# The running sum of the 31-tap convolution on VectorE: in a PSUM bank instead of SBUF

## The chip, the core and the metric

The kernel runs on one core of one Trainium2 chip. The metric is the device time of one execution in microseconds (us); lower is better. TensorE multiplies, VectorE (DVE), ScalarE (ACT) and GpSimd (POOL) do the rest, SyncE (SP) issues most transfers. SBUF is the large on-chip memory, PSUM the smaller one of eight banks into which TensorE writes; one bank holds 128 x 512 numbers of fp32.

## The reference, cut to what matters

Two transformer blocks on 512 tokens of width 1024, in fp32. The change lies in the mixer of the first block, which runs an attention and a convolution side by side on the same normed input:

```python
q = rmsnorm(zq...); k = rmsnorm(zk...)            # 16 query heads, 2 key heads
a = sliding_window_attention(q, k, v, sinks[i]) @ attn_proj[i]
ca, cb = jnp.split(zc, 2, axis=-1)
u = ca * jax.nn.sigmoid(cb)
u = causal_depthwise_conv(u, dw_w[i], dw_b[i])    # 31 taps, each channel by itself
c = jax.nn.silu(layernorm(u, ...)) @ conv_proj[i]
merged = jax.nn.sigmoid(ga) * a + jax.nn.sigmoid(gb) * c
x = x + merged @ w_out[i]
```

For each of the 1024 channels the convolution is y[t] = b + sum over j of w[j] * u[t - 30 + j], 31 products and sums for each token.

## The kernel before

Activations lie with channels on the 128 partitions and the 512 tokens along the free dimension, so 1024 channels are 8 chunks. A weight matrix is used in units of 128 output channels. Each fp32 operand is split into a rounded part h and a rest l, and each product is three matmuls (`mm3`, lines L226 to L228: h by xh, h by xl, l by xh). A unit over 1024 inputs is therefore 24 matmuls of 512 columns. For each unit a weight block arrives in `wst` by a transfer, ScalarE casts it to `wh` (L187) and VectorE subtracts to get `wl` (L188); `wst` has two buffers, `wh` and `wl` have three each.

`mix` is the first mixer. Its units follow each other in the order in which the code is written: keys and values, then for each chunk c of the convolution a unit for cb and one for ca (16 units), then the 8 query chunks and the 8 second gates in turn (`MIX_ORDER`), then the 8 first gates, `attn_proj`, `conv_proj` and `w_out`. TensorE runs exactly in the written order. For VectorE, ScalarE and GpSimd a scheduler fixes the order when the kernel is built; at run time each engine goes through its own list and waits where an operand is not there.

The convolution's input `u` of a chunk is made by VectorE from the ca unit (L758). Then its 31 taps are handed out by `take`: so many at each unit (`FILL`), each not before the first matmuls of that unit. Chunks 0, 3 and 6 (`POOL_CONV`) go to GpSimd: ScalarE scales `u` into `cv` (L650), GpSimd adds it to `y` (L651). Chunks 1, 2, 4, 5 and 7 go to VectorE: one tap is one instruction (L654) that reads `u`, multiplies by a column of `vec` and adds the old `y`, which it reads from SBUF and writes back. Five taps of VectorE go with each of the 16 units, six with each gate unit of `MIX_ORDER`, seven with each first-gate unit. When all chunks are done, `layer_norm` begins.

Beside the 16 units of `MIX_ORDER` the attention runs in rounds, one after each unit (`attention`). A round has up to three parts for three different steps: `attn_c` (L617, probabilities by values, into a bank `sm`), `attn_b` (L604, two groups of transposes into two `pd` banks, each copied out by ScalarE into `pt`, L605) and `attn_a` (two groups of six matmuls of queries by keys into two more `pd` banks, each read by VectorE with the mask, L574; then three instructions on 4 columns, L579 to L581, and four exponentials on ScalarE, L583). Every second round also has the transposes of a query chunk (L516, one `pd` bank). PSUM is shared so: three banks `mm` for the units, one bank `sm`, and four banks `pd`, which the stage takes in turn.

Of the kernel before, what the change touches and what calls it, by code (L numbers as in the profile page):

```python
# [15 lines left out]
P = 128  # L16
S = 512
# [29 lines left out]

# queries and second gates in turn
MIX_ORDER = [0, 1]
# [4 lines left out]

# keys, queries and values of the attention to the memory
XA_ORDER = [("w_xk_2", m) for m in range(3)]
# [49 lines left out]
class Kern:  # L106
# [14 lines left out]

    # ---- tiles
    def nm(self, s):
# [16 lines left out]
    def pd(self):  # L140
        return self.pq.tile([P, S], F32, tag="pd", name=self.nm("pd"), bufs=4)

    def phase(self, name):
        """SBUF and PSUM of one stage; what it returns closes them."""
        ctx = ExitStack()
        self.pm = ctx.enter_context(self.tc.tile_pool(name=name, bufs=1))
        self.pq = ctx.enter_context(self.tc.tile_pool(name=name + "_ps", bufs=1, space=bass.MemoryType.PSUM))
        return ctx
# [12 lines left out]

    # ---- weight stream
    AHEAD_DMA, AHEAD_SPLIT, BOOST, MM = 4, 2, 400, 3
# [40 lines left out]

    # ---- background work
    def tick(self):
# [15 lines left out]

    # ---- matrix products
    def mm3(self, ps, h, l, xh, xl, first, last):
# [22 lines left out]
    def group(self, entries, xs, part, drain=False, fill=0):  # L247
        """Products whose last operands come late: each begins with xs[:part]."""
        begun = []
        for i, (name, m, evac) in enumerate(entries):  # L250
            self.mark(f"{name}/{m}")
            wh, wl = self.w_get(name, m)
            ps = self.mm()
            begun.append((wh, wl, ps, evac))
            for k in range(part):
                sl = slice(k * P, k * P + P)
                self.mm3(ps[:], wh[:, sl], wl[:, sl], *xs[k], k == 0, False)
                if k == 0 and fill:
                    self.take(fill, self.last_mm)
            with self.tc.high_priority(offset=self.BOOST):  # L260
                self.w_prefetch(max(1, min(self.AHEAD_SPLIT, 2 - i)))
            if drain:
                self.tick()
        if drain:
            self.drain()
        for wh, wl, ps, evac in begun:
            for k in range(part, len(xs)):
                sl = slice(k * P, k * P + P)
                self.mm3(ps[:], wh[:, sl], wl[:, sl], *xs[k], False, k == len(xs) - 1)
            with self.tc.high_priority(offset=self.BOOST):  # L270
                self.w_prefetch()
                evac(ps)
            if not drain:
                self.tick()

    def units(self, name, n, xs, first, part, evac, fill=0):
        """n products of one weight, of which some begin before the last operands."""
        if first:
            self.group([(name, m, lambda ps, m=m: evac(m, ps)) for m in range(first)], xs, part, True, fill)
        for m in range(first, n):  # L280
            self.unit(name, m, xs, lambda ps: evac(m, ps), fill=fill)

    # ---- arithmetic pieces
    def split(self, h, l, src, col=None):
# [9 lines left out]
    def rsqrt(self, ps, n, out, N=S, after=None):  # L294
        """out = (ps / n + EPS) ** -0.5: a first value from exp and ln, then a Newton step."""
        nc = self.nc
# [13 lines left out]
    def rsqrt_small(self, v, out, tag, after=None):  # L310
        """out = v ** -0.5 for a few columns."""
        nc = self.nc
# [10 lines left out]
    def preload(self, table, after, before):  # L323
        """Load an activation table between two instructions of ScalarE."""
        ld = self.nc.scalar.preload_act_table_set(table)
        self.order(ld, after)
        self.order(before, ld)
# [7 lines left out]
    def feed(self, acc, x, last, N=S):  # L335
        """Add the squares of one chunk to the accumulator acc (a list that holds its tile)."""
        nc = self.nc
# [16 lines left out]
    def norm_chunk(self, m, gname, last):  # L354
        """x chunk m is final: feed its square, and split x*g for the next product."""
        x = self.x[:, m, :]
# [20 lines left out]
    def lazy_R(self, acc, **k):  # L377
        """R is made where it is first asked for, when a first product is under way."""
        st = []
# [11 lines left out]

    # ---- stages
    def load(self, g0):
        """The first operands come in pieces, and before what only the norm needs."""
        nc = self.nc
# [21 lines left out]
    def ffn(self, tag, gnext, early=False):  # L417
        """early: the squares of x come late, so the first products are held until then."""
        nc = self.nc
# [39 lines left out]

    # ---- first mixer  # L460
    def spill_x(self):
# [28 lines left out]
    def rope_tables(self, a):  # L490
        """cos and sin times the gain of the queries."""
        nc = self.nc
# [6 lines left out]
    def q_chain(self, c, ps):  # L499
        """One chunk of queries without its norm, which q_scales gives to the scores."""  # L500
        nc = self.nc
# [22 lines left out]
    def q_scales(self, grp):  # L524
        """(mean(z^2) + EPS)^-0.5 / 8 for each place and head of a group."""
        nc = self.nc
# [111 lines left out]
    def conv_taps(self, c):  # L638
        """The convolution of one chunk of u, which comes doubled: mix halves the taps."""
        nc = self.nc  # L640
        u, y = self.u.pop(c), self.c5("y")[:, :S]
        w = lambda j: self.vcol("dw_w", c * 31 + j, 1)
        pool = c in self.POOL_CONV
        eng = nc.gpsimd if pool else nc.vector
        yield eng.tensor_scalar(out=y, in0=u[:, 30:542], scalar1=w(30), scalar2=self.vcol("dw_b", c),
                                op0=ALU.mult, op1=ALU.add)
        for j in range(30):
            if pool:
                t = self.t2("cv")
                r = nc.scalar.activation(t[:], u[:, j:j + S], AF.Copy, scale=w(j))  # L650
                eng.tensor_tensor(out=y, in0=y, in1=t[:], op=ALU.add)  # L651
                yield r
            else:
                yield eng.scalar_tensor_tensor(out=y, in0=u[:, j:j + S], scalar=w(j), in1=y,  # L654
                                               op0=ALU.mult, op1=ALU.add)
# [8 lines left out]
    def conv_fill(self, chunks):  # L664
        """The convolution of some chunks, a tap at a time."""
        for c in chunks:
# [4 lines left out]
    def take(self, counts, dep):  # L671
        """Up to so many taps of each filler, not before dep."""
        for fill, n in zip(self.fill, counts):
# [37 lines left out]
    def normed(self, gname, R):  # L711
        """Operands of the normed x itself, so that what its products give needs no scale."""
        nc = self.nc
# [8 lines left out]
    def mix(self, gnext):  # L722
        nc = self.nc
        ctx = self.phase("mixp")
        self.spill_x()
# [85 lines left out]

    # ---- gated embedding
    def ple(self, gnext):
# [33 lines left out]

    # ---- second mixer
    def bc(self, col, n):
        """[P, n] columns, each repeated over 128 places."""  # L850
        return col.rearrange("p (a c) -> p a c", c=1).to_broadcast([P, n, P])
# [51 lines left out]
    def conv4(self, raw, ch, out):  # L903
        """Causal convolution over 4 places of one chunk; raw has 3 zeros ahead."""
        nc = self.nc
# [6 lines left out]
    def token_squares(self, chunk, j):  # L912
        """Sum of one chunk's squares over the channels, a column for each block of 128 places."""
        nc = self.nc
# [11 lines left out]
    def dn_scales(self):  # L926
        """Scales of keys and queries, and what they make of the gates' columns."""
        tt = self.nc.vector.tensor_tensor
# [12 lines left out]
    def dn_chunk(self, n, st):  # L941
        """Decays, inverse of the triangle, and the products that one chunk of 128 places needs."""
        nc = self.nc
# [49 lines left out]
        def halves(t, l, odd):  # L993
            """The columns in even or odd blocks of 2^l."""
            w = 1 << l
# [114 lines left out]
    def dn_out(self, n, po):  # L1110
        """Norm and gate of one chunk's outputs, places on the partitions; then back to channels."""
        nc = self.nc
# [126 lines left out]

    # ---- attention to the memory  # L1240
    def xhead(self, h):
# [41 lines left out]
    def mem_prep(self):  # L1283
        """Operands and norm of the memory; the products that follow need no x."""
        nc = self.nc
# [69 lines left out]

    # ---- squared-relu MLP and the last norm
    def mlp(self):
# [21 lines left out]
    def final(self, hs):  # L1379
        """The last product by halves of the tokens: the norm of one is under way beside the other."""  # L1380
        nc = self.nc
# [73 lines left out]

# ---- host layout
def tile_w(w, k0=0, k1=None):
# [102 lines left out]
```

## Time and profile before

| | us |
|---|---|
| median of three runs | 2098.96 (2096.82 to 2099.27) |
| profiled execution, from its first to its last instruction (span) | 2092.0 |
| median less that span | 6.96 |
| TensorE busy over the span | 2015.6 |
| VectorE busy over the span | 1270.8 |
| first mixer, the part with taps on VectorE | 413.7 to 743.2 of the span |

The time of a run has some microseconds more than the span; the profiled execution has no time of its own beside its span here, so the median stands for it. A matmul's listed duration is longer than its distance to the next one (they overlap in the engine), so TensorE's busy share says little; its counts and the waits of a stretch say more. The three stretches used below are parts of the first mixer: 413.7 to 516.8 us, the units of ca and cb; 516.8 to 677.4 us, queries and second gates with the attention; 677.4 to 743.2 us, first gates with the last rounds of the attention.

### The profile page before, as it was taken

Reading aid. Unit: us, or ns where it says so; the run is one execution under the profiler, and the core shown is the slowest. Engines: PE = TensorE matmul, PEld = TensorE weight load, DVE = VectorE, ACT = ScalarE, POOL = GpSimd, SP = SyncE. Lnnn points to the kernel's source line nnn. Section 1 sums busy time; section 2 is a strip of 40 time slices with the busy share of each in tenths; the row PEclk is TensorE's granted clock in tenths of the full one; section 3 lists DMA queues with packets and bytes.
Section 4 is the critical chain, followed back from the end, with each engine's and each line's share of the span. In section 5 each row is a group of like instructions: output and inputs, shape, how many; then the busy total and the mean of one; then the engine's idle time right before and its main releaser. Section 6 shows DMA issues by size and latency. Waiting matters only on the chain. (4 is left out here: it accounts for less than half of the span.)

```text
span 2092.0 us, 25092 instructions
## 1 busy us (share of the span) xinstructions
PE 2015.6 (96%) x9564; PEld 1676.9 (80%) x9564; DVE 1270.8 (61%) x1956; ACT 876.8 (42%) x1465; POOL 249.3 (12%) x234
## 2 busy tenths in 40 slices
PE   8999999977899799999999999999999999999997
PEld 6888888756778578888888877788988988888886
DVE  6434345899989985544443468678486655344444
ACT  5323223633777652422222255354555444232233
POOL 0000000375223600000000002207100000000001
PEclk9999999998999899999999999999999999999999
DMA  5333333312212134332323224322034333233232
GB/s 178 100 94 98 101 92 122 103 61 71 79 60 79 41 96 132 130 100 92 101 92 100 91 82 145 100 86 72 7 117 146 119 103 101 91 101 97 95 101 71
DMA packets 65672, 201.13 MB, mean 96 GB/s; under 512 B 7312, under 2 KB 11536, under 8 KB 65424
## 3 DMA queue, kind: packets, MB, share of 16 engines
q1 hardware_dynamic: 64864, 199.00, 29.8%
q8 instruction: 76, 1.25, 0.2%
q10 hardware_dynamic: 688, 0.53, 0.1%
q14 instruction: 44, 0.36, 0.1%
HBM read 188.75 MB, written 10.49 MB: 95 GB/s over the span
## 5 line engine op out<-in xcount | busy, mean ns | idle before, releaser
L187 ACT CAST wh<-wst 128x1024 fp32r<-128x1024 f32 (+3 forms) x357 | 353.9, 992 | 934.1 <-PE mm L227 634.3
L226 PE MATMUL mm<-xh,wh 128*128 128x512 f32 x1272 | 502.2, 395 | 2.5 <-ACT xh L290 1.5
L228 PE MATMUL mm<-xh,wl 128*128 128x512 f32 x1272 | 495.9, 390 | 0.7 <-DVE wl L188 0.7
L227 PE MATMUL mm<-xl,wh 128*128 128x512 f32 x1272 | 495.4, 389 | 0.3 <-DVE xl L291 0.3
L188 DVE TENSOR_TENSOR wl<-wst,wh 128x1024 fp32r<-128x1024 f32 (+3 forms) x357 | 420.5, 1179 | 75.4 <-ACT wh L187 75.2
L226 PEld LDWEIGHTS mm<-xh,wh 128*128 128x128 f32 x1272 | 238.9, 188 | 55.0 <-issue 2.9
L227 PEld LDWEIGHTS mm<-xl,wh 128*128 128x128 f32 x1272 | 239.0, 188 | 52.2 <-issue 3.1
L228 PEld LDWEIGHTS mm<-xh,wl 128*128 128x128 f32 x1272 | 238.8, 188 | 51.5 <-DVE wl L188 1.6
L227 PE MATMUL mm<-hl,wh 128*128 128x512 f32 (+1 forms) x616 | 238.3, 387 | 0.2
L226 PE MATMUL mm<-hh,wh 128*128 128x512 f32 (+1 forms) x616 | 238.5, 387 | 0.0
L228 PE MATMUL mm<-hh,wl 128*128 128x512 f32 (+1 forms) x616 | 238.1, 387 | 0.0
L371 DVE SCALAR_TENSOR_TENSOR x<-mm,x 128x512 f32<-128x512 f32 x111 | 76.7, 691 | 248.7 <-PE mm L228 248.7
L651 POOL TENSOR_TENSOR y<-y,cv 128x512 f32<-128x512 f32 x90 | 143.4, 1594 | 158.4 <-ACT cv L650 153.8
L654 DVE SCALAR_TENSOR_TENSOR y<-u,vec,y 128x512 f32<-128x512 f32 x150 | 160.3, 1069 | 2.8
L228 PE MATMUL mm<-xnh,wl 128*128 128x512 f32 x304 | 123.4, 406 | 18.8 <-DVE wl L188 18.8
L227 PEld LDWEIGHTS mm<-hl,wh 128*128 128x128 f32 x616 | 115.7, 188 | 24.3 <-DVE hl L288 1.0
L226 PEld LDWEIGHTS mm<-hh,wh 128*128 128x128 f32 x616 | 115.7, 188 | 23.5
L228 PEld LDWEIGHTS mm<-hh,wl 128*128 128x128 f32 x616 | 115.7, 188 | 23.4
L226 PE MATMUL mm<-xnh,wh 128*128 128x512 f32 x304 | 124.0, 408 | 4.3 <-DVE u L758 3.6
L227 PE MATMUL mm<-xnl,wh 128*128 128x512 f32 x304 | 121.9, 401 | 0.0
L438 DVE TENSOR_TENSOR t<-mm,R 128x512 f32<-128x512 f32 x43 | 29.7, 692 | 138.4 <-PE mm L228 138.3
L228 PEld LDWEIGHTS mm<-xnh,wl 128*128 128x128 f32 x304 | 59.4, 195 | 35.3 <-DVE wl L188 22.4
(403 smaller groups left out, 2807.2 us busy)
## 6 DMA issues: line engine op xcount, KB each, us to landing
wst<-ffn_wgu SPq DMA_DIRECT2D x86, 512.0 KB, 3.5
wst<-w_in SPq DMA_DIRECT2D x63, 512.0 KB, 3.5
wst<-ffn_wdown SPq DMA_DIRECT2D x32, 512.0 KB, 3.5
wst<-w_up SPq DMA_DIRECT2D x32, 512.0 KB, 3.5
wst<-w_down SPq DMA_DIRECT2D x32, 512.0 KB, 3.5
wst<-ffn_wdown SPq DMA_DIRECT2D x16, 384.0 KB, 3.1
xd<-x SPq DMA_DIRECT2D x24, 256.0 KB, 2.3
x<-xd SPq DMA_DIRECT2D x24, 256.0 KB, 4.8
```

The lines of the kernel that those rows point to most:

```text
L187: r = self.nc.scalar.copy(h[:, c], st[:, c])
L188: self.nc.vector.tensor_tensor(out=l[:, c], in0=st[:, c], in1=h[:, c].bitcast(F32), op=ALU.subtract)
L226: self.last_mm = mm(ps, h, xh, start=first, stop=False)
L227: mm(ps, h, xl, start=False, stop=False)
L228: mm(ps, l, xh, start=False, stop=last)
L371: self.nc.vector.scalar_tensor_tensor(out=x, in0=ps[:], scalar=scale, in1=x, op0=ALU.mult, op1=ALU.add)
L438: nc.vector.tensor_tensor(out=t[:], in0=ps[:], in1=R[:], op=ALU.mult)
L651: eng.tensor_tensor(out=y, in0=y, in1=t[:], op=ALU.add)
L654: yield eng.scalar_tensor_tensor(out=y, in0=u[:, j:j + S], scalar=w(j), in1=y, op0=ALU.mult, op1=ALU.add)
```

## The change

On VectorE's five chunks the running sum is a tile `cacc` in PSUM. The first tap writes it, taps 2 to 30 read and write it, the last tap reads it and writes `y` in SBUF, which everything later uses as before. The bank comes from the stage's four `pd` banks, of which three are left in the first mixer; other stages keep four. GpSimd's chunks are as before. (The change also drops comments, which is not shown.)

```diff
     def pd(self):
-        return self.pq.tile([P, S], F32, tag="pd", name=self.nm("pd"), bufs=4)
+        return self.pq.tile([P, S], F32, tag="pd", name=self.nm("pd"), bufs=self.PD)
...
-    def phase(self, name):
...
-        ctx = ExitStack()
+    def phase(self, name, pd=4):
...
+        ctx, self.PD = ExitStack(), pd
...
     def conv_taps(self, c):
...
-        pool = c in self.POOL_CONV
-        eng = nc.gpsimd if pool else nc.vector
-        yield eng.tensor_scalar(out=y, in0=u[:, 30:542], scalar1=w(30), scalar2=self.vcol("dw_b", c),
-                                op0=ALU.mult, op1=ALU.add)
-        for j in range(30):
-            if pool:
...
-            else:
-                yield eng.scalar_tensor_tensor(out=y, in0=u[:, j:j + S], scalar=w(j), in1=y,
+        else:
+            eng = nc.vector
+            acc = self.pq.tile([P, S], F32, tag="cacc", name=self.nm("cacc"), bufs=1)[:]
+            yield eng.tensor_scalar(out=acc, in0=u[:, 30:542], scalar1=w(30), scalar2=self.vcol("dw_b", c),
+                                    op0=ALU.mult, op1=ALU.add)
+            for j in range(30):
+                yield eng.scalar_tensor_tensor(out=y if j == 29 else acc, in0=u[:, j:j + S], scalar=w(j), in1=acc,
                                                op0=ALU.mult, op1=ALU.add)
...
     def mix(self, gnext):
-        ctx = self.phase("mixp")
+        ctx = self.phase("mixp", 3)
```

The scheduler makes new lists for VectorE, ScalarE and GpSimd. First VectorE among the ca and cb units, where it goes from its first to its second chunk. Before:

```order
L654 SCALAR_TENSOR_TENSOR y_2849<-u_2841,vec,y_2849 128x512 x5
L758 SCALAR_TENSOR_TENSOR u_3127<-tcb_3035,mm_3082 128x512
L188 TENSOR_TENSOR wl_3172<-wst_3079,wh_3171 128x1024
L645 TENSOR_SCALAR y_3136<-u_2937,vec 128x512
L757 MEMSET u_3223 128x30
L654 SCALAR_TENSOR_TENSOR y_3136<-u_2937,vec,y_3136 128x512 x5
L188 TENSOR_TENSOR wl_3218<-wst_3125,wh_3217 128x1024
```

After the change, at the same place (lines stand five lower there, so L763 is the old L758):

```order
L659 SCALAR_TENSOR_TENSOR cacc_2850<-u_2841,vec,cacc_2850 128x512 x4
L763 SCALAR_TENSOR_TENSOR u_3128<-tcb_3036,mm_3083 128x512
L659 SCALAR_TENSOR_TENSOR cacc_2850<-u_2841,vec,cacc_2850 128x512
L188 TENSOR_TENSOR wl_3174<-wst_3080,wh_3173 128x1024
L659 SCALAR_TENSOR_TENSOR cacc_2850<-u_2841,vec,cacc_2850 128x512
L659 SCALAR_TENSOR_TENSOR y_2849<-u_2841,vec,cacc_2850 128x512
L762 MEMSET u_3225 128x30
L656 TENSOR_SCALAR cacc_3138<-u_2938,vec 128x512
L659 SCALAR_TENSOR_TENSOR cacc_3138<-u_2938,vec,cacc_3138 128x512 x2
L188 TENSOR_TENSOR wl_3220<-wst_3126,wh_3219 128x1024
```

The mix of taps and `wl` is the same, about five taps to a `wl`; the order shifts by a tap or two, and 58 taps stand ahead of the first query chunk in both lists.

Second TensorE in one round of the attention, whose order does not change but whose waits do (the name in brackets is the engine waited for). `pd` tiles are in the order two of `attn_b`, two of `attn_a`. Before:

```order
L604 MATMUL pd_4219<-cst,s_4025 128x128 [waits DVE_49] x2
L604 MATMUL pd_4225<-cst,s_4025 128x128 [waits Activation_49]
L604 MATMUL pd_4225<-cst,s_4025 128x128 x3
L226 MATMUL pd_4233<-kph,qh_3417 128x256 [waits DVE_49]
L227 MATMUL pd_4233<-kpl,qh_3417 128x256
L228 MATMUL pd_4233<-kph,ql_3418 128x256
L226 MATMUL pd_4242<-kph,qh_3417 128x256 [waits DVE_49]
```

After:

```order
L604 MATMUL pd_4222<-cst,s_4028 128x128 [waits DVE_49]
L604 MATMUL pd_4228<-cst,s_4028 128x128 [waits Activation_49]
L604 MATMUL pd_4228<-cst,s_4028 128x128 x3
L226 MATMUL pd_4236<-kph,qh_3419 128x256 [waits DVE_49]
L227 MATMUL pd_4236<-kpl,qh_3419 128x256
L228 MATMUL pd_4236<-kph,ql_3420 128x256
L226 MATMUL pd_4245<-kph,qh_3419 128x256 [waits Activation_49]
```

With four banks the second half of `attn_a` waited for VectorE, which had read the same bank a round earlier. With three it takes the bank of the round's own first `attn_b` transposes, so it waits for ScalarE to have copied them out.

## Rows read from the trace of the kernel before

**Rows 1.** The page: its first line, and all taps of VectorE (busy us, mean ns).

```profile
span 2092.0 us, 25092 instructions
...
L654 DVE SCALAR_TENSOR_TENSOR y<-u,vec,y 128x512 f32<-128x512 f32 x150 | 160.3, 1069 | 2.8
```

**Rows 2.** Busy time by stretch: start and end, length, then each engine.

```profile
core 0: us, PE busy (x) PEld busy (x) DVE busy (x) ACT busy (x) POOL busy (x), PEclk, DMA share, GB/s
413.70:516.80 103.10, 80.75 (x303) 62.25 (x302) 100.87 (x87) 38.80 (x56) 68.59 (x42) 0.88 0.20 61
516.80:677.40 160.60, 149.10 (x798) 128.14 (x797) 147.49 (x362) 120.07 (x271) 46.05 (x32) 0.98 0.23 75
677.40:743.20 65.80, 50.74 (x215) 40.65 (x213) 62.69 (x88) 36.28 (x77) 37.39 (x24) 0.90 0.15 47
...
410.50:427.00 16.50, 16.50 (x73) 13.44 (x73) 16.32 (x14) 9.67 (x14) 15.79 (x10) 1.00 0.21 64
```

**Rows 3.** Waits of TensorE, 413 to 517 us: total, times, longest.

```profile
PE mm L228 <- DVE wl L188: 18.8, 8, 5.8
```

**Rows 4.** Waits of TensorE, 516.8 to 677.4 us.

```profile
PE pd L516 <- ACT pt L605: 5.7, 4, 2.3
PE pd L604 <- ACT s L590: 3.2, 1, 3.2
```

**Rows 5.** Waits of TensorE, 677.4 to 743.2 us.

```profile
PE sm L617 <- ACT pt L605: 7.6, 2, 3.9
```

**Rows 6.** Groups of VectorE, 413.7 to 516.8 us: busy us, mean ns.

```profile
L654 DVE SCALAR_TENSOR_TENSOR y<-u,vec,y 128x512 f32<-128x512 f32 x58 | 72.6, 1252 | 1.6
L188 DVE TENSOR_TENSOR wl<-wst,wh 128x1024 fp32r<-128x1024 f32 x13 | 24.1, 1850 | 0.7 <-ACT wh L187 0.7
L758 DVE SCALAR_TENSOR_TENSOR u<-tcb,mm 128x512 f32<-128x512 f32 x6 | 4.1, 680 | 0.0
```

**Rows 7.** Timeline of VectorE about 430 us: start, us, what.

```profile
427.91 1.65 DVE L654 SCALAR_TENSOR_TENSOR y<-u,vec,y 128x512 f32<-128x512 f32 x1
429.48 0.67 DVE L758 SCALAR_TENSOR_TENSOR u<-tcb,mm 128x512 f32<-128x512 f32 x1
...
431.16 2.28 DVE L188 TENSOR_TENSOR wl<-wst,wh 128x1024 fp32r<-128x1024 f32 x1
```

**Rows 8.** Timeline of GpSimd: 17 additions without a gap.

```profile
407.56 30.39 POOL L651 TENSOR_TENSOR y<-y,cv 128x512 f32<-128x512 f32 x17
```

**Rows 9.** Durations of two lines: ns least/median/most.

```profile
L574 DVE CUSTOM_DVE_ANT_0 s<-pd,cst x64: 403/418/426, 535.8 to 703.9; 128x256 f32<-128x256 f32 x64
L291 DVE SCALAR_TENSOR_TENSOR xl<-x,vec,xh x56: 742/747/755, 5.1 to 1731.2; 128x512 fp32r<-128x512 f32 x56
L291 DVE SCALAR_TENSOR_TENSOR yp<-pd,vec,yp x4: 739/742/746, 1326.9 to 1343.5; 128x512 fp32r<-128x512 f32 x4
L654 DVE SCALAR_TENSOR_TENSOR y<-u,vec,y x150: 719/752/1880, 413.7 to 738.7; 128x512 f32<-128x512 f32 x150
```

**Rows 10.** Timeline of VectorE: three taps that follow each other.

```profile
509.94 2.31 DVE L654 SCALAR_TENSOR_TENSOR y<-u,vec,y 128x512 f32<-128x512 f32 x3
```

**Rows 11.** Groups of VectorE, 677.4 to 743.2 us.

```profile
L654 DVE SCALAR_TENSOR_TENSOR y<-u,vec,y 128x512 f32<-128x512 f32 x38 | 40.2, 1058 | 0.8
L188 DVE TENSOR_TENSOR wl<-wst,wh 128x1024 fp32r<-128x1024 f32 x7 | 8.6, 1235 | 2.2 <-ACT wh L187 2.2
L581 DVE TENSOR_TENSOR st<-st,vec 128x4 f32<-128x4 f32 x3 | 3.7, 1249 | 0.0
```

**Rows 12.** Timeline of TensorE in one round of the attention.

```profile
613.26 1.04 PE L604 MATMUL pd<-cst,s 128*128 128x128 f32 x8
...
614.85 0.28 PE L226 MATMUL pd<-kph,qh 128*128 128x256 f32 x1
```

**Rows 13.** Timeline of ScalarE in the same round: both copies.

```profile
615.65 1.06 ACT L605 COPY pt<-pd 128x512 f32<-128x512 f32 x2
```

**Rows 14.** Waits of all engines, 400 to 800 us.

```profile
ACT s L583 <- DVE st L580: 30.0, 15, 2.9
```

More of the change, by code (lines that the diff above doesn't have):

```diff
@@ L642, in conv_taps @@
         w = lambda j: self.vcol("dw_w", c * 31 + j, 1)
-        pool = c in self.POOL_CONV
-        eng = nc.gpsimd if pool else nc.vector
-        yield eng.tensor_scalar(out=y, in0=u[:, 30:542], scalar1=w(30), scalar2=self.vcol("dw_b", c),
-                                op0=ALU.mult, op1=ALU.add)
-        for j in range(30):
-            if pool:
+        if c in self.POOL_CONV:
+            eng = nc.gpsimd
+            yield eng.tensor_scalar(out=y, in0=u[:, 30:542], scalar1=w(30), scalar2=self.vcol("dw_b", c),
+                                    op0=ALU.mult, op1=ALU.add)
+            for j in range(30):
                 t = self.t2("cv")
@@ L652, in conv_taps @@
                 yield r
-            else:
-                yield eng.scalar_tensor_tensor(out=y, in0=u[:, j:j + S], scalar=w(j), in1=y,
+        else:
+            eng = nc.vector
+            acc = self.pq.tile([P, S], F32, tag="cacc", name=self.nm("cacc"), bufs=1)[:]
+            yield eng.tensor_scalar(out=acc, in0=u[:, 30:542], scalar1=w(30), scalar2=self.vcol("dw_b", c),
+                                    op0=ALU.mult, op1=ALU.add)
+            for j in range(30):
+                yield eng.scalar_tensor_tensor(out=y if j == 29 else acc, in0=u[:, j:j + S], scalar=w(j), in1=acc,
                                                op0=ALU.mult, op1=ALU.add)
```

## The prediction

> **What bounds the kernel now.** TensorE's busy share is high everywhere and tells little, so I read the table of stretches first [rows 2]. Where nothing holds it, TensorE starts a matmul every 16.50 / 73 = 0.226 us, so a unit of 24 takes 5.4 us. From 413.7 to 516.8 us (stretch A) 303 matmuls would need 303 x 0.226 = 68.5 us, and the stretch takes 103.1. VectorE is busy for 100.87 of these. [...] In the first-gate stretch (C, 677.4 to 743.2 us) VectorE is busy for 62.69 of 65.8 us, and TensorE waits for `pt` [rows 5], whose copies stand in ScalarE's list behind exponentials that wait for VectorE [rows 14]. In between (stretch B) VectorE is busy for 147.49 of 160.6 us, but TensorE loses less: 5.7 us of it for a `pd` bank that ScalarE has not yet copied out, and 3.2 us for probabilities [rows 4]. So VectorE sets the pace in A and C and is nearly full in B.
>
> Then I looked for what fills VectorE. A tap takes 752 ns in the median and up to 1880 [rows 9]; in A the mean is 1252 and `wl`'s 1850 [rows 6]. The timeline shows why: from 407.56 us on, GpSimd adds without a gap for 30.39 us [rows 8], and inside that time VectorE's taps take 1.65 and `wl` 2.28 us, while L758, which has one input in SBUF and the other in PSUM, takes its usual 0.67 us between them [rows 7]. The slow instructions have two inputs in SBUF. L574, with a PSUM input and the mask in SBUF, shows the same over 64 instructions: 403 to 426 ns, whatever GpSimd did [rows 9].
>
> [...]
>
> **The change part by part.** *A tap beside GpSimd.* It reads `u` in SBUF and the sum in PSUM, so by L758 and L574 it should not be held. *A tap alone.* Three taps that depend on each other take 2.31 us, so one starts (2.31 - 0.75) / 2 = 0.78 us after the other [rows 10]. With a PSUM input the same instruction form takes 742 ns against 747 with SBUF [rows 9], so reading PSUM costs nothing. Writing PSUM from VectorE occurs nowhere in this trace. From below I bound a tap by 0.68 us (L758, which has no column of scalars); from above by a read and a write of one bank that can't go on together: the 512 elements once more at L758's pace, 0.78 + 0.68 = 1.46 us at most. I take 0.78, because every form on VectorE that differs only in one PSUM operand has the same time.
>
> [...]
>
> *Stretch A.* 58 taps: 72.6 us become 58 x 0.78 = 45.2, which takes 27 us off VectorE. `wl` keeps two SBUF inputs: its 13 took 24.1 us [rows 6], and at C's mean of 1.235 us [rows 11] they would take 16.1. GpSimd still has its three additions per unit, so I leave `wl` at 24.1, the upper end, and count the possible 8 us in the range. VectorE's 100.9 becomes about 74; with the same 2.2 us of idle time the stretch is 76 us long, a gain of 27. TensorE's own need of 68.5 stops the gain at 34.6. With taps at 0.85 it is 23, and static lists that wait on each other could take a few more: 19 to 34.
>
> *Stretch C.* 38 taps, 40.2 us, become 38 x 0.78 = 29.6: 10.6 less. The small L581 has two SBUF inputs and takes 1.25 us for 4 columns [rows 11], and L579 and L580 before it are of the same kind; the change does not free them, though GpSimd may be done sooner. VectorE was busy 95% of C, so most comes through: 10, between 5 and 14.
>
> *Stretch B.* 55 taps: VectorE is relieved too, by about 55 x (0.86 - 0.78) = 4.4 us (of the 160.3 us of all 150 taps [rows 1], 72.6 in A and 40.2 in C leave 47.5 for 55, 0.86 each). Against it stands the bank. `pd` is taken in the order `attn_b` twice, `attn_a` twice; with three banks the second half of `attn_a` needs the first of `attn_b`'s, and the built program waits for ScalarE there, where before it waited for VectorE, long done. In one round the transposes start at 613.26, the second half of `attn_a` at 614.85 [rows 12], but ScalarE copies the first bank only at 615.65 and the second by 616.71 [rows 13]; a copy is about half of 1.06, so the bank is free at 616.2: a wait of 1.4 us that was not there. B has 13 rounds with both parts (8 transposes each); if this one is typical, 13 x 1.4 = 18 us. The 5.7 us that the query transposes now wait for these same copies [rows 4] would be gone, since they come later: 12 us net. Queued behind the waiting matmuls are the next unit's, and so everything. But the copies are late because ScalarE's list has the exponentials of the round before ahead of them, and those wait 30.0 us in all for VectorE's L580 [rows 14]. A VectorE that runs early brings them forward, and a TensorE that waits lets both catch up. I cannot price that from rows. I take 0 for B, between 12 lost and 10 gained (the waits of [rows 4], 8.9 us, and a little clock).
>
> The first tap of each chunk (five) loses nothing that counts, one bank for all chunks makes VectorE wait only for itself, and the last tap writes `y` as before. After C comes `layer_norm`, whose results are wanted eight units of `attn_proj` later (8 x 5.4 = 43 us); it moves with the last tap.
>
> Sum: 27 + 0 + 10 = 37 us. From the profiled span of 2092.0 [rows 1] that is 2055, and with the 6.96 us that the median has over this span, **2062 us**.
>
> **The rivals.** *1. The bank eats a good part.* In B the copies stay as late as they are: 12 us lost, gain 25, 2074 us. For it: ScalarE's copy comes late in nearly every round. Against: see above. *2. All of VectorE's lateness was the taps.* A comes down to TensorE's 68.5 (35 us), B gains 8, C 14: 2042 us. Against: `wl` and the small instructions still meet GpSimd. *3. A tap that reads and writes one PSUM bank is slow* (the case on the other side). At 1.46 us, A has 58 x 1.46 = 85 for taps instead of 72.6, 12 us more; B 55 x 0.6 = 33 more VectorE work on 147.5, of which 13 fit in its idle time, so 20; C 38 x 0.4 = 15. Together 47 us slower, 2146. It decides where a tap costs more than about 1.07 us, its mean now [rows 1]. No row shows VectorE writing PSUM, so nothing but the equal times of reads speaks against it. *4. The change doesn't do what it says*: taps are held beside GpSimd whatever they read, because they write or because of `u`. Then taps stay as they are and the bank costs up to 12: 2099 to 2111. L758 and L574 speak against it. *5. A tap in PSUM is dearer by a little*: if the write and the next tap's read of it add a tenth of the bound's 0.68, 0.07 us, A loses 58 x 0.07 = 4 of its gain, C 3, and B's 4 mostly fit in its idle time: 2069 us. For it: each tap waits for the one before, so a later write shows in full. Against: reads show nothing of the kind.
>
> **How the numbers follow.** Chances: the forecast 0.49, rival 1 0.19, rival 2 0.10, rival 3 0.08, rival 4 0.04, rival 5 0.10. The forecast's own range, from A's 19 to 34 and C's 5 to 14, is 2051 to 2075. To hold 8 in 10 I reach on one side to rival 2, on the other past rival 1 with A at its lower end (19 + 10 - 12 = 17 gained, 2082): 2043 to 2084. A difference under 0.2%, about 4 us, can't be told from none in this kernel. Faster is the forecast with rivals 1, 2 and 5, 0.88; slower rival 3 and half of rival 4, 0.10; the same 0.02.
>
> **What would show it.** Taps with one narrow duration near 0.75 us, started 0.78 us apart, also beside GpSimd's additions; GpSimd's additions shorter than now; stretch A near 76 us with the granted clock up; in B waits of `pd` L226 for `pt` L605, some 1 us each, where there are none now; C near 56 us. Wrong it would be made by a tap over 1 us, by B longer by more than 12 us, or by A still paced by `wl` near 2.3 us each.

## The result, and the profile after

The changed kernel takes 2047.58 us (median of four runs, 2045.61 to 2047.88), the kernel before on the same chip 2098.11 (2096.82 to 2099.27): a ratio of 0.976, 95% interval 0.9749 to 0.9772, 50.5 us faster. The prediction was 2062 us with a range of 2043 to 2084. Its sign and its mechanism held. Its terms for A and C were too small, and B, taken at 0, came out 5.5 us longer. The time also lies below the forecast's own range of 2051 to 2075 us.

The taps first: duration of all 150 (ns least/median/most), then GpSimd's additions. Lines from the taps on stand five lower than before.

```profile
L659 DVE SCALAR_TENSOR_TENSOR cacc<-u,vec,cacc x145: 719/756/757, 413.7 to 689.7; 128x512 f32<-128x512 f32 x145
L659 DVE SCALAR_TENSOR_TENSOR y<-u,vec,cacc x5: 731/742/748, 447.8 to 690.5; 128x512 f32<-128x512 f32 x5
...
L651 POOL TENSOR_TENSOR y<-y,cv x90: 1264/1297/2284, 408.3 to 681.6; 128x512 f32<-128x512 f32 x90
```

No tap is longer than 757 ns, where one had taken up to 1880 [rows 9]; the median hardly moved, because what is gone is the long half. GpSimd is held less too: 1297 ns in the median of its additions, where it was 1620. The timelines of VectorE and GpSimd at the place of [rows 7, 8] show that the taps are short beside the additions too:

```profile
428.09 1.26 DVE L188 TENSOR_TENSOR wl<-wst,wh 128x1024 fp32r<-128x1024 f32 x1
429.27 3.91 DVE L659 SCALAR_TENSOR_TENSOR cacc<-u,vec,cacc 128x512 f32<-128x512 f32 x5
433.09 0.68 DVE L763 SCALAR_TENSOR_TENSOR u<-tcb,mm 128x512 f32<-128x512 f32 x1
433.69 2.05 DVE L188 TENSOR_TENSOR wl<-wst,wh 128x1024 fp32r<-128x1024 f32 x1
...
412.48 29.43 POOL L651 TENSOR_TENSOR y<-y,cv 128x512 f32<-128x512 f32 x18
```

Five taps in 3.91 us start (3.91 - 0.75) / 4 = 0.79 us apart, while GpSimd adds all the time; `wl`, with two SBUF inputs, takes 1.26 and 2.05 us here.

The same work by stretch, in the columns of [rows 2]. Each table's first row is A with the units ahead of the first tap, so all 16 units of ca and cb; its last is B and C together. Before:

```profile
394.10:516.80 122.70, 99.66 (x385) 77.56 (x384) 117.89 (x108) 53.75 (x76) 82.47 (x50) 0.90 0.21 67
516.80:743.20 226.40, 199.84 (x1010) 168.79 (x1008) 210.18 (x448) 156.35 (x348) 83.44 (x55) 0.95 0.21 67
```

After, with B and C also one by one:

```profile
394.70:482.70 88.00, 87.31 (x385) 71.97 (x384) 83.83 (x105) 54.48 (x76) 79.22 (x51) 1.00 0.28 93
482.70:648.80 166.10, 153.84 (x797) 131.36 (x796) 148.96 (x374) 128.63 (x287) 45.74 (x34) 0.96 0.22 72
648.80:694.90 46.10, 44.17 (x214) 36.92 (x212) 42.84 (x77) 30.33 (x62) 28.99 (x21) 1.00 0.20 67
482.70:694.90 212.20, 198.00 (x1009) 168.28 (x1007) 191.80 (x450) 158.96 (x349) 74.74 (x54) 0.97 0.22 71
```

A lost 34.7 us and is now TensorE's: 16 units in 88.0 us are 5.5 us each, the granted clock is 1.00, and no wait for `wl` is left, where it was 18.8 us [rows 3]. C lost 19.7. B became 5.5 us longer. Ahead of A 0.6 us were lost, and behind C 1.9, so the span of 2045.6 is 46.4 below that of before. The waits of TensorE in B:

```profile
PE pd L226 <- ACT pt L605: 4.6, 3, 2.2
PE pd L226 <- DVE st L574: 4.2, 2, 2.8
PE pd L604 <- ACT s L590: 2.2, 1, 2.2
```

One round of them, first TensorE, then ScalarE:

```profile
545.10 1.04 PE L604 MATMUL pd<-cst,s 128*128 128x128 f32 x8
...
549.09 0.39 PE L226 MATMUL pd<-kph,qh 128*128 128x256 f32 x1 [2.24 <-ACT pt L605]
...
546.45 1.04 ACT L187 CAST wh<-wst 128x1024 fp32r<-128x1024 f32 x1
547.38 0.91 ACT L590 ACTIVATE s<-s,st 128x256 f32<-128x256 f32 x2
548.20 0.36 ACT L287 CAST qh<-sm 128x256 fp32r<-128x256 f32 x1
548.45 1.08 ACT L605 COPY pt<-pd 128x512 f32<-128x512 f32 x2
```

The transposes are done by 546.1, and ScalarE copies them out at 548.45, because a cast of weights, two scalings and another cast, 2.3 us in all, stand ahead in its list. TensorE has to wait for the first copy, as predicted for the third bank.

### The profile page after: what moved, and what is told of

It reads as the page before. It is cut to its first block, busy times and chain, and to the rows that moved or that the text cites. A ratio compares the mean times of both kernels' runs of the same rounds, so it can differ in the third digit from the quotient of the medians.

```text
span 2045.6 us, 25091 instructions
## 1 busy us (share of the span) xinstructions
PE 2004.0 (98%) x9564; PEld 1672.0 (82%) x9564; DVE 1218.2 (60%) x1956; ACT 881.0 (43%) x1467; POOL 237.5 (12%) x234
## 5 line engine op out<-in xcount | busy, mean ns | idle before, releaser
L651 POOL TENSOR_TENSOR y<-y,cv 128x512 f32<-128x512 f32 x90 | 131.8, 1464 | 126.0 <-ACT cv L650 109.1
L438 DVE TENSOR_TENSOR t<-mm,R 128x512 f32<-128x512 f32 x43 | 29.7, 691 | 138.4 <-PE mm L228 138.3
L659 DVE SCALAR_TENSOR_TENSOR cacc<-u,vec,cacc 128x512 f32<-128x512 f32 x145 | 108.9, 751 | 2.8
L432 DVE TENSOR_TENSOR t<-mm,R 128x512 f32<-128x512 f32 x43 | 29.7, 691 | 94.1 <-PE mm L228 94.0
```

The lines of the kernel that those rows point to most:

```text
L432: nc.vector.tensor_tensor(out=t[:], in0=ps[:], in1=R[:], op=ALU.mult)
L438: nc.vector.tensor_tensor(out=t[:], in0=ps[:], in1=R[:], op=ALU.mult)
L659: yield eng.scalar_tensor_tensor(out=y if j == 29 else acc, in0=u[:, j:j + S], scalar=w(j), in1=acc, op0=ALU.mult, op1=ALU.add)
```

## The experiments

Each kernel was timed against the kernel before on the same chip; ratios are to it, with 95% intervals. "B and C" is the time from the first transposes of queries to the first product of `layer_norm`: 226.4 us before, 212.2 after.

**The bank alone.** The changed kernel with three `pd` banks, but the sum in SBUF:

```diff
-            acc = self.pq.tile([P, S], F32, tag="cacc", name=self.nm("cacc"), bufs=1)[:]
+            acc = y
```

> The first mixer has three banks pd instead of four, but the running sum stays in SBUF as before (the fourth bank is not used). Theory, that the third bank is what cost B its 5.5 us and more, since VectorE's relief is missing here: A and C as before (122.7 us for the 16 units of ca and cb with their front, 65.8 for C), taps held as before (mean 1069 ns), B longer by 6 to 18 us with waits of pd L226 for pt L605, 2104 to 2116 us in all. Rival, that B's loss in the changed kernel comes from the new order of VectorE's list (two more wl in B) and not from the bank: B within 2 us of 160.6, time within 0.2% of 2098.

Measured: 2096.82 us, 0.9998 (0.9989 to 1.0007): no change. Waits of TensorE over B and C:

```profile
PE pd L226 <- ACT pt L605: 17.3, 11, 5.4
```

The windows of B and of C:

```profile
518.00:690.10 172.10, 151.65 (x798) 129.38 (x797) 154.39 (x370) 126.95 (x288) 55.91 (x38) 0.97 0.22 70
690.10:745.70 55.60, 48.78 (x214) 40.36 (x213) 52.31 (x78) 28.77 (x59) 26.17 (x17) 0.91 0.17 56
```

B is 11.5 us longer. Ten of the waits, 14.2 us, lie in B, and the query transposes wait 0.3 us for these copies instead of 5.7 [rows 4]; that is 8.8 us net, and the other 2.7 are not accounted for. But C is 10.2 us shorter: while TensorE waits for the bank, VectorE goes on with its list (154.39 us of work in B instead of 147.49), and C has less to do (52.31 instead of 62.69). With VectorE as the bound, B and C are one stretch, and the waits of TensorE inside it cost nothing in the end. The theory was right on where the bank costs and how much there, and wrong on the total; the rival was right on the total, and wrong on B.

**Which operand counts.** The tap with only its read, then with only its write in PSUM:

```diff
-                yield eng.scalar_tensor_tensor(out=y if j == 29 else acc, in0=u[:, j:j + S], scalar=w(j), in1=acc,
+                yield eng.scalar_tensor_tensor(out=y, in0=u[:, j:j + S], scalar=w(j), in1=acc,
```

```diff
-            yield eng.tensor_scalar(out=acc, in0=u[:, 30:542], scalar1=w(30), scalar2=self.vcol("dw_b", c),
+            yield eng.tensor_scalar(out=y, in0=u[:, 30:542], scalar1=w(30), scalar2=self.vcol("dw_b", c),
...
-                yield eng.scalar_tensor_tensor(out=y if j == 29 else acc, in0=u[:, j:j + S], scalar=w(j), in1=acc,
+                yield eng.scalar_tensor_tensor(out=y if j == 29 else acc, in0=u[:, j:j + S], scalar=w(j), in1=y,
```

> As the changed kernel, but only the read of the sum is in PSUM: each tap reads cacc, as the first tap left it, and writes y in SBUF (so the 29 sums are not carried on). Theory, that what matters is the number of SBUF inputs: taps near 0.75 us also beside GpSimd's additions, A near 88 us, C near 46, time within 5 us of the changed kernel's 2047.6. Rival, that the write to SBUF holds a tap too: taps of 1.2 us in the mean in A, time 2080 us or more.

> The other half: each tap reads u and y in SBUF and writes cacc in PSUM (so the sums are not carried on). Theory, two SBUF inputs: taps held as before, mean near 1.05 us (about 1.25 in A), and with three banks the time of the kernel with the bank alone, 2100 to 2116 us. Rival, that the write to SBUF was what GpSimd held: taps near 0.75 us, time near 2048.

Measured: 2046.49 us, 0.9761 (0.9747 to 0.9776), and 2097.34, 1.0001 (0.9992 to 1.001). Durations of the taps, first of the one that reads PSUM:

```profile
L659 DVE SCALAR_TENSOR_TENSOR y<-u,vec,cacc x150: 706/748/752, 413.0 to 689.0; 128x512 f32<-128x512 f32 x150
```

and of the one that writes it:

```profile
L659 DVE SCALAR_TENSOR_TENSOR cacc<-u,vec,y x145: 721/760/1847, 414.0 to 739.7; 128x512 f32<-128x512 f32 x145
```

The whole gain is in the second input's place. The write matters neither way. The order of VectorE's list does not explain it: over A, taps and `wl` follow each other much alike in both of these, with five or six taps to a `wl`. In neither run are the sums carried on from tap to tap through PSUM; that this costs nothing is shown by the changed kernel itself, with 0.79 us from tap to tap.

**GpSimd's additions left out**, from the kernel before and from the changed one:

```diff
-                eng.tensor_tensor(out=y, in0=y, in1=t[:], op=ALU.add)
```

> The kernel before, four banks, sum in SBUF, without GpSimd's 90 additions of its chunks (left out of the computation; ScalarE still makes cv). Theory, that GpSimd's additions are what holds VectorE: no tap over 0.8 us, wl near 1.2 us, A near TensorE's floor of 87 to 88 us, C 45 to 48, B 150 to 158 (four banks and a freer VectorE), so about 2098 - 35 - 19 - 5 = 2039 us, 2032 to 2046. Rival, that part of the changed kernel's gain comes from PSUM itself or from the new order: taps narrow, but A or C stays 5 us or more above the changed kernel's 88.0 and 46.1 us, time over 2050.

> The changed kernel (sum in PSUM, three banks) without GpSimd's 90 additions (left out of the computation; ScalarE still makes cv). The twin with four banks and the sum in SBUF took 2026.5 us: A 88.4, B 147.7, C 44.2, each from the first product of a unit of the stretch to that of the next. Theory, that with VectorE free of GpSimd the third bank is what is left to pay in B: A and C as there, B 6 to 12 us longer, by waits of pd L226 for pt L605, so 2032 to 2039 us. Rival, that the lists hide the missing bank once VectorE has time (ScalarE copies early): B 147 to 150, 2026 to 2029 us. Then the 18 us that B has above this in the changed kernel are GpSimd's hold on wl and the small instructions, not the bank.

Measured: 2026.47 us, 0.9664 (0.9651 to 0.9677), and 2033.14, 0.9691 (0.9677 to 0.9706). A is 88.0 us in both. B and C, four banks with the sum in SBUF:

```profile
482.50:630.60 148.10, 145.63 (x798) 126.15 (x797) 132.42 (x373) 124.98 (x287) 6.31 (x4) 1.00 0.24 77
630.60:674.30 43.70, 43.70 (x214) 37.02 (x213) 37.62 (x73) 29.00 (x61) 4.17 (x3) 1.00 0.22 69
```

and three banks with the sum in PSUM:

```profile
483.20:635.90 152.70, 146.79 (x797) 126.48 (x796) 132.71 (x373) 128.24 (x289) 6.30 (x4) 1.00 0.23 75
635.90:679.70 43.80, 43.80 (x214) 37.11 (x213) 37.29 (x72) 29.15 (x62) 3.88 (x3) 1.00 0.22 68
```

So the additions, which are GpSimd's work and not VectorE's, cost the kernel before 2098.2 - 2026.5 = 71.7 us. The change gets 50.5 of it back. The additions still cost the changed kernel 2047.6 - 2033.1 = 14.5 us. Over B and C VectorE is busy for 191.80 us with them and 170.01 without. Of these 21.8 us, 16.2 are the four instructions on 4 columns (L579 to L581 and L586, 26.8 us against 10.6), and only 3.0 are `wl` (31.9 against 28.9). L579 with the additions, then without:

```profile
L579 DVE SCALAR_TENSOR_TENSOR st<-st,qsc 128x4 f32<-128x4 f32 x16 | 7.0, 437 | 0.0
```

```profile
L579 DVE SCALAR_TENSOR_TENSOR st<-st,qsc 128x4 f32<-128x4 f32 x16 | 2.4, 153 | 0.0
```

That the 14.5 us come from these instructions is inferred from VectorE's time; no run frees them alone. And once VectorE is free, the missing bank does cost something: 2033.14 - 2026.47 = 6.7 us, though the two intervals touch. 4.7 of it lie in B and C, where TensorE waits 3.4 us for `pt` and 2.3 for L574 before `attn_a`; with four banks it waits only 2.3 us, for the query transposes. The time is within what was expected; B's 4.6 are below the 6 to 12. The first kernel came out 5.5 us under its range, for its B and C took 191.8 us where the theory had 226.4 - 24 = 202.4.

**Another order in a round**, so that no matmul needs a bank from ScalarE in the same round: `attn_a`, `attn_c`, `attn_b`, and `attn_c`, `attn_a`, `attn_b`. The edit of the first (the second keeps `attn_c` in front):

```diff
+            new = []
+            if steps and steps[0][0] in self.q_r:
+                new = [[0, steps[0], self.attn_a(*steps.pop(0))]]
             for e in live:
...
-            live = [e for e in live if e[0] < 3]
-            if steps and steps[0][0] in self.q_r:
-                live.append([0, steps[0], self.attn_a(*steps.pop(0))])
+            live = [e for e in live if e[0] < 3] + new
```

> The changed kernel with another order in a round of the attention: attn_a, attn_c, attn_b instead of attn_c, attn_b, attn_a. With three banks the second transposes of attn_b now need the bank that VectorE (L574) has read in the same round, 3 us earlier on TensorE, and no matmul needs a bank that ScalarE has to copy out in the same round. Theory, that the wait for ScalarE's copy is what B loses: B 165.7 down to 152 to 160 us, 2034 to 2043 us, no waits of pd L226 for pt L605. Rival, that VectorE's time is what B is made of (149 of 166 us busy, the rest scattered): B stays within 3 us, 2045 to 2051 us, and the waits move to pd L604 for s.

> As the run before, but with the order attn_c, attn_a, attn_b: attn_c stays first, and the second transposes of attn_b come 1.3 us after the bank's matmuls instead of 3. Theory: between the changed kernel and the run before, 2036 to 2046 us, with waits of pd L604 for DVE (st or s, L574). Rival, as there: 2045 to 2051.

Measured: 2067.21 us, 0.9853 (0.9836 to 0.9869), and 2065.75, 0.9846 (0.9831 to 0.9861): 18 to 20 us slower than the changed kernel. Both expectations fell, theory and rival. The waits of TensorE in the first, 480 to 760 us (19.7 us in 14 for the same in the second):

```profile
PE pd L604 <- ACT pt L605: 20.1, 14, 3.6
```

One round of it:

```profile
548.19 0.60 PE L604 MATMUL pd<-cst,s 128*128 128x128 f32 x4
549.52 0.66 PE L604 MATMUL pd<-cst,s 128*128 128x128 f32 x4 [0.73 <-ACT pt L605]
```

I had read the code wrongly. `attn_b` of a round belongs to the step of two rounds ago, and `s` has two buffers: an `attn_a` that is written ahead of it needs the buffer that these transposes have still to read. So L574 can't read the banks of `attn_a` before the transposes, these can't have such a bank, and the second group of transposes got the bank of the first and waits for its copy, 14 times. The waits are shown, the way to them is read from the code. A third buffer of `s` was not tried.

**The sum in PSUM only in A and C** (chunks 1, 2 and 7); for chunks 4 and 5 it is in SBUF, and every fourth `pd` takes the bank:

```diff
+        if self.PD == 3 and self.free and self.np % 4 == 0:
+            return self.pq.tile([P, S], F32, tag="cacc", name=self.nm("pd"), bufs=1)
...
+            bank = c in self.SUMS
+            acc = self.pq.tile([P, S], F32, tag="cacc", name=self.nm("cacc"), bufs=1)[:] if bank else y
+            self.free = not bank
...
+    LN_WAIT, SUMS = 6, (1, 2, 7)
```

> The running sum is in PSUM only for chunks 1, 2 (all taps of A and the first of B) and 7 (the last 30 taps, in C); for chunks 4 and 5, whose taps lie in B and at C's beginning, it is in SBUF and the bank serves as a fourth pd. Theory, that the bank costs more than PSUM saves in B: A 88.4, B 155 to 162, C 47 to 52, 2040 to 2049 us. Rival, that B and C together are VectorE's time, as the kernel with the bank alone showed (B 11.5 us longer, C 10.2 shorter, 2096.8 in all): the held taps of chunks 4 and 5 (about 0.12 us each beside additions) show, 2050 to 2058 us.

Measured: 2054.61 us, 0.9794 (0.9779 to 0.9808), 7.0 slower than the changed kernel; B and C take 219.2 us. The rival held. The taps of chunks 4 and 5, then those of 7 and the rest of 2:

```profile
L665 DVE SCALAR_TENSOR_TENSOR y<-u,vec,y 128x512 f32<-128x512 f32 x60 | 54.1, 902 | 0.6
L665 DVE SCALAR_TENSOR_TENSOR cacc<-u,vec,cacc 128x512 f32<-128x512 f32 x30 | 22.5, 751 | 0.6
```

60 x (0.902 - 0.751) = 9 us of VectorE's time weigh more than the bank did in this form. It is not quite a fourth `pd` bank: it is taken at fixed turns, and one wait of 5.7 us for a copy is left.

**`attn_a` half a unit later**, which needs no other buffer; `late` is called in the middle of the next unit. In the first of two runs, on the changed kernel, the three banks are also taken strictly in turn:

```diff
+        if self.PD == 3:
+            self.np += 1
+            return self.pq.tile([P, S], F32, tag="pd%d" % (self.np % 3), name=self.nm("pd"), bufs=1)
...
+            if k == nb // 2 and self.late:
+                self.late()
+                self.late = None
...
-                live.append([0, steps[0], self.attn_a(*steps.pop(0))])
+                e = [0, steps.pop(0), None]
+                live.append(e)
+                self.late = lambda: e.__setitem__(2, self.attn_a(*e[1]))
```

> The changed kernel (same attn_c, attn_b order, two buffers s), but attn_a of a round is issued in the middle of the next unit, 2.7 us after attn_b, and the three banks pd are taken strictly in turn. So the bank that attn_a needs from attn_b's transposes has had half a unit to be copied out. Theory, that B's wait for the round's own copies is worth about what the third bank costs with VectorE free (B 152.3 against 147.7 us): B 165.7 down to 156 to 162, no wait of pd L226 for pt L605 over 1 us, 2038 to 2044 us. Rival, that in B the waits for banks only stand in for VectorE's and ScalarE's own lateness (the chain from L574 over the exponentials to the transposes): the waits move to pd L604 for s, B 164 to 170, 2046 to 2052 us, since the chain also starts half a unit later.

> The same shift of attn_a into the middle of the next unit in the kernel before (four banks, sum in SBUF). Theory, that VectorE sets the pace of A and of B and C together there: within 0.2% of 2098. Rival, that the shift is a gain or a loss by itself, whatever the sum's place: 4 us or more from 2098, and then the run above is to be read against this.

Measured: 2056.9 us, 0.9807 (0.9794 to 0.9821), and 2104.25, 1.0034 (1.0021 to 1.0048). Waits of TensorE over B and C in the first (its lines stand four to seven lower):

```profile
PE pd L611 <- DVE st L581: 9.3, 6, 2.9
PE pd L230 <- DVE st L581: 4.7, 1, 4.7
PE pd L611 <- ACT s L597: 3.2, 1, 3.2
...
PE pd L230 <- ACT pt L612: 0.3, 1, 0.3
```

The waits for copies are gone, and the time with them is not: waits for VectorE's L574 (L581 here) stand in their place, and B and C take 220.5 us. The rival was nearer, but its numbers missed too: the time is 5 us above its range, and only 3.7 us of the waits are for `s`. The test is blunt as well, since the shift costs 6.2 us by itself in the kernel before. What is shown is that no gain came of removing the bank's wait in this way.

**VectorE's time against ScalarE's in B and C**, by who scales the four probability blocks of a round: `NORM_ACT` of them go to ScalarE, 3 in the first run, shown here, and 1 in the second.

```diff
-    NORM_ACT = 2
+    NORM_ACT = 3
```

> The changed kernel with three instead of two of the four probability blocks of a round normalised on ScalarE (L590) and one instead of two on VectorE (L592): in 16 rounds 16 x 0.42 = 6.7 us less for VectorE and 16 x 0.50 = 8 us more for ScalarE. Theory, that B and C together are VectorE's time (191.8 us busy of 212.2): B and C 4 to 7 us shorter, 2040 to 2044 us. Rival, that it is ScalarE's list, in which copies and exponentials stand late, that sets B: 2047 to 2056 us.

> The opposite: one block on ScalarE, three on VectorE, 6.7 us more for VectorE and 8 less for ScalarE. Theory: 4 to 7 us longer, 2051 to 2055 us. Rival: 2040 to 2047 us.

Measured: 2051.18 us, 0.9779 (0.9766 to 0.9792), and 2045.94, 0.9752 (0.9739 to 0.9766). B and C of the first, then of the second:

```profile
482.60:700.10 217.50, 200.78 (x1009) 170.97 (x1008) 185.30 (x432) 161.25 (x363) 72.40 (x54) 0.95 0.22 69
```

```profile
481.90:691.70 209.80, 196.46 (x1010) 167.37 (x1009) 192.72 (x464) 152.24 (x333) 73.93 (x54) 0.98 0.22 72
```

The theory that VectorE alone paces B and C after the change fell: with 6.5 us less work on VectorE and 2.3 more on ScalarE they are not 4 to 7 us shorter, but 5.3 longer in the profiled execution and 3.6 in the medians. The opposite gives 1.6 us in the medians. Neither difference of medians can be told from none; the two runs together, 5.2 us apart, go against the theory, and both times lie in the rival's ranges. The second is a weak test of it, for VectorE's work rose by only 0.9 us, not 6.7. What VectorE waits for ScalarE at L586, 8.2 us in the changed kernel, moves with ScalarE's work, in the first run and in the second:

```profile
L586 DVE TENSOR_TENSOR st<-st 128x4 f32<-128x4 f32 x16 | 4.0, 252 | 10.5 <-ACT st L585 10.5
```

```profile
L586 DVE TENSOR_TENSOR st<-st 128x4 f32<-128x4 f32 x16 | 5.7, 359 | 0.7 <-ACT st L585 0.6
```

So ScalarE's list ends some of the waits now; how much it and VectorE's are worth stays open. No version here that computes everything is measurably better than the changed kernel.

## Why the prediction was right or wrong

- **A tap at 0.78 us, not held: right.** 0.75 us long, 0.79 apart, also beside GpSimd. The read alone gives the whole gain, so rival 4 is out. In the changed kernel each tap reads the bank that the tap before wrote, and starts 0.79 us after it, where it was 0.78 in SBUF [rows 10]; so rivals 3 and 5 are out. The 0.85 us for a tap that rival 5 and one end of A's range reckon with no run shows: in the changed kernel 757 ns is the most. The read of PSUM took no longer either: 748 ns in the median where only the read is in PSUM, against 752 in SBUF in the kernel without additions. But the reason given, that forms which differ in one PSUM operand take the same time, rested on one pair [rows 9] and does not hold for the first tap: 0.54 us alone into SBUF, 0.80 into PSUM.
- **The gain in A, 27 us: mis-sized, it was 34, at the upper end of the 19 to 34 given.** From the first tap to the first query A took 69.0 us (413.7 to 482.7) instead of the 76 I had. Its VectorE groups:

```profile
L659 DVE SCALAR_TENSOR_TENSOR cacc<-u,vec,cacc 128x512 f32<-128x512 f32 x57 | 42.9, 753 | 1.6
L188 DVE TENSOR_TENSOR wl<-wst,wh 128x1024 fp32r<-128x1024 f32 x13 | 21.6, 1659 | 0.0
```

  `wl` I had left at 24.1 us; it took 21.6. GpSimd's additions became shorter too (1297 ns against 1620 in the median) and were sooner out of the way (the last starts at 681.6 us instead of 725.3), which may be why. The taps with the one that writes `y` took 43.6 where I had 45.2; the first tap fell from 1.5 to 0.8 us; and the first query chunk's rotation (2.0 us), which stood at the end of the stretch before, came behind it. These are 6.8 us, and with them A came to the limit of 34.6 that the prediction had named, within half a microsecond.
- **0 for B and 10 for C: each mis-sized, and the cut between them was the mistake.** B lost 5.5, C gained 19.7, more than the 5 to 14 given; together 14.2 instead of 10. The run with the bank alone shows why they can't be priced apart: work of VectorE moves from one to the other when TensorE waits. In the sum over both, before and after:

```profile
L654 DVE SCALAR_TENSOR_TENSOR y<-u,vec,y 128x512 f32<-128x512 f32 x92 | 87.7, 953 | 1.2
L188 DVE TENSOR_TENSOR wl<-wst,wh 128x1024 fp32r<-128x1024 f32 x23 | 28.5, 1240 | 7.7 <-ACT wh L187 7.7
```

```profile
L659 DVE SCALAR_TENSOR_TENSOR cacc<-u,vec,cacc 128x512 f32<-128x512 f32 x88 | 65.9, 749 | 1.3
L188 DVE TENSOR_TENSOR wl<-wst,wh 128x1024 fp32r<-128x1024 f32 x23 | 31.9, 1385 | 3.4 <-ACT wh L187 3.4
```

  With the last taps (3.0 us for 4) the taps took 18.8 us less; `wl` took 3.4 us more. VectorE's busy time went from 210.2 to 191.8 us, and the time from 226.4 to 212.2.
- **The third bank, 18 us of waits and 12 net (rival 1's loss): right for B, wrong for the kernel.** The bank alone gave 17.3 us of waits (14.2 in B) and made B 11.5 longer, and 0 in the end. That "a TensorE that waits lets both catch up" was a reason given for not subtracting it, and it held. So did the other, that a VectorE that runs early brings the copies forward: in the changed kernel the waits for `pt` are 4.6 us in B, three of them, against 14.2 in ten with the bank alone.
- **Rival 2 came nearest** (A 35, B 8, C 14; 2042 us): A was its 34.7, B and C 14.2 of its 22. Without additions B and C take 191.8 us with four banks and 196.5 with three; so the rest is, as far as the runs show, GpSimd's hold on VectorE, its small instructions above all, and the bank. Rival 2 had a chance of 0.10, so that the time lies in the stated range is owed to the reach that was given to it, and not to the forecast's sizes.
- **The sum.** 46.4 us of span were gained, not 37: 7.7 more in A, 4.2 in B and C, 2.5 lost ahead and behind. The other 5 us of the error come from the 6.96 us beside the span: the changed kernel's own run has 1.8 (2047.42 with a span of 2045.6), and every other run with its span on record, of the kernel before too, has 1.7 to 1.9. So the profiled execution of before was one of its faster ones, of about 2094 us, and its span was no base for the median. The stretches of before are then 4 to 5 us short in all, and where is not known.

## What to carry to other kernels

In this mixer, where GpSimd adds too, a tap with two SBUF inputs took 719 ns at the least, 752 in the median and 1880 at the most [rows 9], and with one of them in PSUM 757 at the most: look at least, median and most of a line before its mean, and see whether a form with a PSUM input is free of the long ones. Moving the second input to PSUM was worth 50 us here, and the bank that it took cost nothing by itself (a ratio of 0.9998), with VectorE as the bound. Stretches that one engine paces belong together: price the sum of its work over all of them, and don't subtract a wait of another engine inside them until a run with the wait alone has shown its cost at the end (here 17.3 us of waits, and 0 in the end).

## What the runs showed of the hardware that was not expected

The first tap of a chunk has one tensor input only, and still took 1.52 us in the median (least 0.53) as long as it wrote SBUF; without GpSimd's additions the median is 0.54, with one of five still at 1.52. In the kernel before, the three of 1.52 us start (at 412.16, 466.94 and 527.04 us) inside additions of GpSimd of 1.64 to 1.68 us, which start at 411.76, 466.50 and 526.60. But of the two of 0.53, one (at 693.11) also has additions beside it, from 691.42 to 693.16 and from 693.24 on. Into PSUM the first tap takes 0.80 to 0.81 us. One SBUF input was thus not always enough to be free of GpSimd for this form; what sets it apart from L758, which took 0.67 us between held taps [rows 7], no run shows. Before, after, and the kernel before without additions:

```profile
L645 DVE TENSOR_SCALAR y<-u,vec x5: 530/1517/1523, 412.2 to 693.1; 128x512 f32<-128x512 f32 x5
```

```profile
L656 DVE TENSOR_SCALAR cacc<-u,vec x5: 801/803/814, 412.9 to 653.7; 128x512 f32<-128x512 f32 x5
```

```profile
L645 DVE TENSOR_SCALAR y<-u,vec x5: 534/541/1521, 410.3 to 633.5; 128x512 f32<-128x512 f32 x5
```

And in one round more time went with a wait of TensorE than its length. Around the wait of 2.24 us in the section on the result, the granted clock (the column behind the engines) was 1.00 up to the end of the wait, and then 0.57 and 0.55 in the mean, for 3.9 us in which matmuls ran without a gap. The six matmuls of `attn_a` ahead of the wait start within 0.68 us, the six behind it within 1.01. That the wait brought the clock down is not shown:

```profile
544.00:546.90 2.90, 2.85 (x20) 2.45 (x18) 2.85 (x9) 2.87 (x6) 0.00 (x0) 1.00 0.00 0
546.90:549.10 2.20, 0.01 (x1) 0.01 (x1) 2.20 (x3) 2.20 (x6) 0.00 (x0) 1.00 0.32 119
549.10:551.10 2.00, 2.00 (x11) 2.00 (x11) 1.88 (x9) 0.43 (x1) 0.00 (x0) 0.57 0.68 174
551.10:553.00 1.90, 1.90 (x7) 1.54 (x6) 1.10 (x5) 1.53 (x3) 0.18 (x1) 0.55 0.23 93
```
